# A diffusion transformer block with 32 experts on one core: an eighth ring area for the weight stream, and GpSimd's four DMAs on ScalarE's queue

## The chip, the core and the metric

The kernel runs on one core of one Trainium2 chip. A core has five engines with queues of their own: TensorE (PE in the profile; PEld is its weight loads), VectorE (DVE), ScalarE (ACT), GpSimd (POOL) and SyncE (SP), which here only issues DMAs. They work on the on-chip memory SBUF (128 partitions) and on the accumulators in PSUM; 16 DMA engines move data between SBUF and the memory outside. The metric is the device time of one execution in microseconds, lower is better.

## What is computed

One block on 256 tokens with 1024 features, in float32: modulation vectors from a condition, attention of two kinds over the tokens and 256 context tokens, and then a mixture of 32 experts. Cut to what matters here:

```python
sh1, sc1, g1, sh2, sc2, g2 = split(silu(c) @ w_mod + b_mod, 6)
h  = modulate(rms_norm(x, norm1_g), sh1, sc1)
p  = h @ w_in                              # q, k, v and gates; k and v of the context too
x  = x + g1 * merge_branches(global_attn(...), window_attn(...), gates, w_br_a, w_br_b, w_o)
h2 = modulate(rms_norm(x, norm2_g), sh2, sc2)
logits = h2 @ w_router + b_router          # top 4 of 32, softmax over the four: combine
for e in range(32):
    u = h2 @ w_e1[e] + b_e1[e]             # 1024 x 2048
    u_glu, u_lin = minimum(u[:, 0::2], 7), clip(u[:, 1::2], -7, 7)
    act = u_glu * sigmoid(1.702 * u_glu) * (u_lin + 1)
    out = out + combine[:, e:e+1] * (act @ w_e2[e] + b_e2[e])    # 1024 x 1024
return rms_norm(x + g2 * out, final_g)
```

The weights of the experts are 32 x 12 MB of float32, and each is read once.

## The kernel before, in words

Everything is one program in an order written out by hand. All large weights go through one **stream**: the list `pieces` names them in the order of their use, each piece a block of 128 partitions by 8 KB (1024 KB in all; half of that for `w_q`), an expert being eight pieces of `w1` and four of `w2`. `areas` holds `N_PAIR` SBUF tiles `ring0`, `ring1` and so on, of 16 KB per partition; each is two halves, and a half takes one piece. `pump` (L85 to L112) issues pieces on SyncE's queue as long as a half is in the list `spare`; `done` puts the half of a used piece back at the list's end and pumps again. So a piece's DMA waits, on SyncE, for the last reader of the piece whose half it takes, and SyncE works strictly in the order of the list. After attention two more tiles, `xx` and `ptt`, are free and join the areas (`grow`), four halves more.

The stages, with their use of the stream: the first modulation products and the q projection (`w_m0`, `w_q`), the other projections with the modulation sums on VectorE, GpSimd and ScalarE (`w_in`, `w_mod`; `mod_v`, `mod_p`, `mod_a`), attention head by head, the merge of the branches (`w_br`, `br_prod`), the output projection with the router's statistics (`w_o`, L692 to L723), the router (L732 to L793), and then the experts: `gather` picks the up to 64 tokens of an expert by a matmul, `gemm1` multiplies with `w1`, `act` computes the activation on VectorE and ScalarE in `tmp4`, `act_turn` transposes it, `gemm2` multiplies with `w2`, its result is scaled by `g2` (a row of 1024 numbers that stands in all partitions), and `scatter` adds it to the tokens. The matmuls of expert `e+1` start before those of `w2` of expert `e`. `settle` (L906) adds the experts' output biases `be2` once, during expert 5. The last two experts have an order of their own, in halves; among them stands a branch (`tc.If`, L1017) with a second path for experts that are chosen by more than 64 tokens. The final norm uses the row `fg`.

Small things have other queues. ScalarE's queue loads constants, x once more (L620), the router's weights and the biases `be1`. GpSimd's queue has four DMAs, for which its descriptors take a scratch in SBUF: `g2`, computed across partitions as `g2t` (8 x 128), is written to memory (L645) and read back as one row into all partitions (L726, into `r_kv`, 128 x 1024); `be2` (L729, into `mtx`, 128 x 512) and `fg` (L730, 128 x 1024) are loaded. In the queue of an engine a DMA stands among its computations, in program order.

DMAs of SyncE and ScalarE signal their end on eight semaphores, DMAHW0 to DMAHW7, given out in turn over both queues; a DMA waits until the one that had its semaphore before has landed, so at most eight are in flight. GpSimd's have others (DMASW).

Three small uses of a 2 KB buffer with the tag `msb` belong to the change: the products `bt` in `settle` and in the branch's path, and `g2x`, the two halves of `g2` put on top of each other for the last experts.

Of the kernel before, what the change touches and what calls it, by code (L numbers as in the profile page):

```python
# [7 lines left out]
F32 = mybir.dt.float32  # L8
# [13 lines left out]
LIMIT = 7.0  # L22
BIG = 1024.0
LOW = -3.0e38
N_PAIR = 7


C_ID, C_IOTA, C_SEL, C_BD2, C_COS, C_SIN, C_TRI, C_MK, C_END = 0, 128, 192, 194, 196, 452, 708, 836, 1092
# [6 lines left out]
def tile_dit_block(ctx: ExitStack, tc: tile.TileContext, xcT, consts, small, rows,  # L35
                   w_m0, w_q, w_mod, w_in, w_br, w_o, w_r, w1, b1, w2, b2, out):
    nc = tc.nc
    ctx.enter_context(tc.manual_schedule())
    per = ctx.enter_context(tc.tile_pool(name="per", bufs=1))
# [36 lines left out]

    areas = [per.tile([128, 4096], F32, name=f"ring{i}") for i in range(N_PAIR)]
    spare = [(i, h) for i in range(N_PAIR) for h in range(2)]
    n_next = [0]
    held, place = {}, {}  # L80

    def half(a):
        return areas[a[0]][:, 2048 * a[1]:2048 * a[1] + 2048]
# [482 lines left out]
    g2_dram = dram.tile([1, 1024], F32, name="g2_dram")  # L566
# [17 lines left out]
    for u in range(8):  # L584
        for qt in range(2):
# [9 lines left out]
            else:  # L595
                for m in (2 * qt, 2 * qt + 1):
                    tag, bufs = (("mm", 1), ("s", 2))[m % 2]
# [44 lines left out]
    nc.tensor.transpose(gp2[0:8, 0:128], modb[:, 24:32], ident)  # L642
    g2t = moe.tile([8, 128], F32, name="g2t", tag="SW", bufs=1)
    nc.vector.tensor_copy(g2t, gp2[0:8, 0:128])
    nc.gpsimd.dma_start(out=g2_dram.rearrange("o (b p) -> (o b) p", b=8), in_=g2t)  # L645
    g1h = moe.tile([128, 8], F32, name="g1h")
    nc.vector.tensor_scalar(out=g1h, in0=modb[:, 0:8], scalar1=0.5, scalar2=None, op0=ALU.mult)
    sh2 = modb[:, 8:16]
# [74 lines left out]
    stats(*pend)  # L723
    g2, fg = r_kv[:, 0:1024], r_kv[:, 1024:2048]
    tmp4 = r_q.rearrange("p (a c) -> p a c", a=4)
    nc.gpsimd.dma_start(out=g2, in_=g2_dram[0:1, :].to_broadcast([128, 1024]))  # L726

    be2 = mtx[:, 0:2, :].rearrange("p a b -> p (a b)")
    nc.gpsimd.dma_start(out=be2, in_=b2)  # L729
    nc.gpsimd.dma_start(out=fg, in_=rows[0:1, 1024:2048].to_broadcast([128, 1024]))  # L730

    nc.scalar.activation(out=junk, in_=eps, func=AF.Exp)  # L732
    u0 = bias1(0)
# [40 lines left out]
    x_t, y_t = t8[0].rearrange("p (a c) -> p a c", a=2), [t8[1].rearrange("p (a c) -> p a c", a=2)]  # L774
# [113 lines left out]
    def scatter(p, tbs=(0, 1)):  # L888
        t, y = TT[p], YY[p]
        for tb in tbs:  # L890
            for h in range(2):
                s = slice(512 * h, 512 * h + 512)
                sp = ps2.tile([128, 512], F32, name="sp", tag="sp", bufs=2)
                nc.tensor.matmul(sp, t[:, tb, :], y[:, s], start=True, stop=True)  # L894
                nc.vector.tensor_tensor(out=ACC[0][:, tb, s], in0=ACC[0][:, tb, s], in1=sp, op=ALU.add)  # L895
# [10 lines left out]
    def settle():  # L906

        ctp = ps2.tile([128, 512], F32, name="ctp", tag="tp")
        cw = mtx[:, 2, :].rearrange("p (a b) -> p a b", a=2)
        combT = mtx[:, 3, :]  # L910
        nc.gpsimd.memset(cw, 0.0)
        for h in range(2):
            nc.gpsimd.tensor_copy(cw[:, :, 64 * h:64 * h + 32], comb)
        for tb in range(2):
            nc.tensor.transpose(ctp[:, 128 * tb:128 * tb + 128], cw[:, tb, :], ident)
        nc.vector.tensor_copy(combT, ctp[:, 0:256])
        for tb in range(2):
            for h in range(2):
                s = slice(512 * h, 512 * h + 512)
                bp = ps2.tile([128, 512], F32, name="bp", tag="xg", bufs=2)  # L920
                nc.tensor.matmul(bp, combT[64 * h:64 * h + 64, 128 * tb:128 * tb + 128], be2[64 * h:64 * h + 64, :], start=True, stop=True)
                t = per.tile([128, 512], F32, name="bt", tag="msb")
                nc.vector.tensor_tensor(out=t, in0=bp, in1=g2[:, s], op=ALU.mult)
                nc.vector.tensor_tensor(out=ACC[0][:, tb, s], in0=ACC[0][:, tb, s], in1=t, op=ALU.add)

# [24 lines left out]
    for e in range(NE - 2):  # L950
        p, j = divmod(e, 2)
# [47 lines left out]
    aT = act_turn(e0)  # L999
    half1(0, 1, u)  # L1000
    scatter(NE // 2 - 2, (1,))
    g2x = per.tile([128, 512], F32, name="g2x", tag="msb")
    for h in range(2):
        nc.vector.tensor_copy(g2x[64 * h:64 * h + 64, :], g2[64 * h:64 * h + 64, 512 * h:512 * h + 512])
    gemm2(e0, aT)
# [11 lines left out]
    with tc.If(cnt > CAP):  # L1017
# [9 lines left out]
        slots = [half(s) for s in spare]  # L1027
# [10 lines left out]
        def body(e):  # L1038
# [11 lines left out]
            for tb in range(2):  # L1050
                aT = y_t[0][:, tb, :].rearrange("p (k s) -> p k s", k=8)
                for ch in range(4):
# [4 lines left out]
                    t = tmp4  # L1057
# [19 lines left out]
            for tb in range(2):  # L1077
                aT = y_t[0][:, tb, :].rearrange("p (k s) -> p k s", k=8)
                for h in range(2):
                    s = slice(512 * h, 512 * h + 512)  # L1080
                    y = ps2.tile([128, 512], F32, name="yd", tag="y")
                    for k in range(8):
                        nc.tensor.matmul(y, aT[:, k, :], vs[k // 2][:, k % 2, s], start=(k == 0), stop=(k == 7))
                    t = per.tile([128, 512], F32, name="bt", tag="msb")
                    nc.vector.tensor_tensor(out=t, in0=y, in1=g2[:, s], op=ALU.mult)
                    nc.vector.scalar_tensor_tensor(out=ACC[0][:, tb, s], in0=t, scalar=cv[:, tb:tb + 1],
                                                   in1=ACC[0][:, tb, s], op0=ALU.mult, op1=ALU.add)

        with tc.For_i(0, NE, 1) as e:
            body(e)  # L1090
# [144 lines left out]
```

## Time and profile before

| | us |
|---|---|
| median of 3 runs (lowest, highest) | 1224.25 (1223.93, 1226.63) |
| the profiled execution, its own time | 1224.82 |
| its span | 1223.0 |
| TensorE busy | 1159.1 (95%) |
| VectorE, ScalarE, GpSimd busy | 359.1, 138.8, 35.2 |
| moved by DMA | 458.36 MB, of it 454.06 MB on SyncE's queue |

The span is from the first to the last instruction of the profiled execution; 1.82 us of its time lie around it. A busy TensorE is not TensorE at its peak, since the ends of its matmuls are modelled. In the views below, L835 is line 835 of the kernel, `PE u L835` is the engine, the tile written and the line, an arrow points from what waited to what ended its wait, and a number in brackets behind an event is the idle time of its engine just before it. PEq, SPq and ACTq are the instruction queues of these engines, where DMA issues and branches appear.

### The profile page before, as it was taken

Reading aid. Unit: us, or ns where it says so; the run is one execution under the profiler, and the core shown is the slowest. Engines: PE = TensorE matmul, PEld = TensorE weight load, DVE = VectorE, ACT = ScalarE, POOL = GpSimd, SP = SyncE. Lnnn points to the kernel's source line nnn. Section 1 sums busy time; section 2 is a strip of 40 time slices with the busy share of each in tenths; the row PEclk is TensorE's granted clock in tenths of the full one; section 3 lists DMA queues with packets and bytes.
Section 4 is the critical chain, followed back from the end, with each engine's and each line's share of the span. In section 5 each row is a group of like instructions: output and inputs, shape, how many; then the busy total and the mean of one; then the engine's idle time right before and its main releaser. Section 6 shows DMA issues by size and latency. Waiting matters only on the chain. (4 is left out here: it accounts for less than half of the span.)

```text
span 1223.0 us, 13639 instructions
## 1 busy us (share of the span) xinstructions
PE 1159.1 (95%) x5624; PEld 529.7 (43%) x5624; DVE 359.1 (29%) x765; ACT 138.8 (11%) x304; POOL 35.2 (3%) x29
## 2 busy tenths in 40 slices
PE   7999999999999999999999999999999899999987
PEld 5888666883343334343434323232323232323222
DVE  3263665332222242322222222222222222222212
ACT  2122553030000000000000000000000000000002
POOL 0231100000000000000000000000000000000000
PEclk9999999999999999999999999999999999999997
DMA  9976655838999999999999999999999999999992
GB/s 379 377 296 212 235 206 201 342 134 361 422 421 421 421 420 421 421 421 421 421 421 422 421 421 421 421 421 421 421 421 421 420 421 421 421 421 421 414 391 75
DMA packets 70066, 458.36 MB, mean 375 GB/s; under 512 B 7848, under 2 KB 8240, under 8 KB 16752
## 3 DMA queue, kind: packets, MB, share of 16 engines
q1 hardware_dynamic: 68304, 454.06, 90.9%
q10 hardware_dynamic: 1296, 2.06, 0.5%
q0 software_dynamic: 400, 1.32, 0.3%
q8 instruction: 46, 0.75, 0.2%
q14 instruction: 20, 0.16, 0.0%
HBM read 456.36 MB, written 1.05 MB: 374 GB/s over the span
## 5 line engine op out<-in xcount | busy, mean ns | idle before, releaser
L835 PE MATMUL u<-ring,t 128*64 128x512 f32 x1488 | 346.0, 600 | 21.7 <-DMA ring<-w 21.7
L835 PEld LDWEIGHTS u<-ring,t 128*64 128x64 f32 x1488 | 99.5, 137 | 223.8 <-issue 162.9
L871 PE MATMUL y<-ring,r_q 128*64 128x512 f32 x832 | 184.2, 593 | 0.0
L884 DVE TENSOR_TENSOR t<-y,r_kv 64x512 f32<-64x512 f32 x60 | 41.3, 689 | 325.6 <-PE y L871 325.2
L871 PEld LDWEIGHTS y<-ring,r_q 128*64 128x64 f32 x832 | 59.3, 137 | 119.6 <-issue 115.8
L845 DVE TENSOR_SCALAR r_q<-u 128x512 f32<-128x512 f32 x31 | 21.4, 692 | 244.0 <-PE u L835 244.0
L835 PE MATMUL u<-ptt,t 128*64 128x512 f32 x320 | 75.6, 598 | 4.4 <-DMA ptt<-w 4.4
L847 ACT ACTIVATE r_q<-r_q 128x512 f32<-128x512 f32 x31 | 19.5, 630 | 505.8 <-DVE r_q L845 505.8
L688 PE MATMUL u<-mtx,keep 128*64 128x512 f32 x256 | 62.2, 604 | 3.0 <-DVE r_q L848 3.0
L805 PEld LDWEIGHTS xg<-mtx,r_y 128*128 128x128 f32 x512 | 58.4, 192 | 12.2 <-issue 12.2
L805 PE MATMUL xg<-mtx,r_y 128*128 128x128 f32 x512 | 61.3, 278 | 0.0
L368 PE MATMUL mm<-xx,ring 128*128 128x256 f32 x256 | 59.9, 385 | 0.0
L894 PE MATMUL sp<-t,mtx 128*128 128x512 f32 x120 | 59.7, 620 | 0.0
L368 PEld LDWEIGHTS mm<-xx,ring 128*128 128x128 f32 x256 | 47.3, 190 | 12.6 <-issue 5.0
L807 DVE TENSOR_TENSOR t<-xg,modb 128x512 f32<-128x512 f32 x32 | 22.1, 692 | 91.1 <-PE xg L805 91.1
L835 PE MATMUL u<-xx,t 128*64 128x512 f32 x176 | 40.4, 596 | 3.7 <-DMA xx<-w 3.7
L835 PEld LDWEIGHTS u<-ptt,t 128*64 128x64 f32 x320 | 21.6, 136 | 48.3 <-issue 34.4
L895 DVE TENSOR_TENSOR r_t<-r_t,sp 128x512 f32<-128x512 f32 x60 | 38.4, 681 | 5.1 <-PE sp L894 5.1
L894 PEld LDWEIGHTS sp<-t,mtx 128*128 128x128 f32 x120 | 20.5, 191 | 39.5 <-issue 39.5
L871 PE MATMUL y<-xx,r_q 128*64 128x512 f32 x160 | 36.3, 594 | 0.0
L688 PEld LDWEIGHTS u<-mtx,keep 128*64 128x64 f32 x256 | 16.3, 135 | 44.6 <-issue 22.6
L861 ACT COPY r_q<-ta 128x512 f32<-128x512 f32 x31 | 18.1, 585 | 145.5 <-PE ta L858 145.5
(245 smaller groups left out, 894.7 us busy)
## 6 DMA issues: line engine op xcount, KB each, us to landing
ring<-w SPq DMA_DIRECT2D x290, 1024.0 KB, 19.8
xx<-w SPq DMA_DIRECT2D x42, 1024.0 KB, 19.8
ptt<-w SPq DMA_DIRECT2D x40, 1024.0 KB, 19.8
ring<-w_mod SPq DMA_DIRECT2D x16, 1024.0 KB, 6.8
ring<-w_in SPq DMA_DIRECT2D x10, 1024.0 KB, 8.7
ring<-w SPq DMA_DIRECT2D x20, 512.0 KB, 11.8
ring<-w_m SPq DMA_DIRECT2D x8, 1024.0 KB, 12.5
ring<-w_q SPq DMA_DIRECT2D x8, 512.0 KB, 12.3
```

Of the source, the lines that this page charges most:

```text
L368: nc.tensor.matmul(gp[0][:, 0:256], w[:, k, :], x[:, k, :], start=(k == 0), stop=(k == 7))
L688: nc.tensor.matmul(u[c0:c0 + 64, ch % 2, :], ident[:, 4 * e + ch:4 * e + ch + 1].to_broadcast([128, 64]), be1, start=True, stop=False)
L805: nc.tensor.matmul(xp[:, b, :], z[:, tb, 128 * k:128 * k + 128], S[:, tb, :], start=(tb == 0), stop=(tb == 1))
L807: nc.vector.tensor_tensor(out=XT[p][:, 4 * h:4 * h + 4, :], in0=xp, in1=sh2[:, 4 * h:4 * h + 4].unsqueeze(2).to_broadcast([128, 4, 128]), ...
L835: nc.tensor.matmul(u[c0:c0 + 64, ch % 2, :], XT[p][:, k, 64 * j:64 * j + 64], w[:, 512 * ch:512 * ch + 512], start=False, stop=(k == 7))
L845: nc.vector.tensor_scalar(out=glu.rearrange("p (b f) -> p b f", b=2), in0=v[:, :, 0, :], scalar1=LIMIT, scalar2=None, op0=ALU.min)
L847: nc.scalar.activation(out=sg, in_=glu, func=AF.Sigmoid, scale=ALPHA)
L861: nc.scalar.copy(out=aT, in_=tp)
L871: nc.tensor.matmul(y[64 * h:64 * h + 64, :], l, w[:, 512 * h:512 * h + 512], start=(k == 0), stop=(k == 7))
L884: nc.vector.tensor_tensor(out=YY[p][64 * j:64 * j + 64, 512 * h:512 * h + 512], in0=y[64 * h:64 * h + 64, :], in1=g2[64 * h:64 * h + 64, 5 ...
L894: nc.tensor.matmul(sp, t[:, tb, :], y[:, s], start=True, stop=True)
L895: nc.vector.tensor_tensor(out=ACC[0][:, tb, s], in0=ACC[0][:, tb, s], in1=sp, op=ALU.add)
```

## The change

`N_PAIR` goes from 7 to 8, which gives the stream an eighth area of 16 KB per partition, so 16 halves in place of 14, and 20 in place of 18 with `xx` and `ptt`. The room comes from the scratch for GpSimd's descriptors, which the builder is told to make 1024 bytes, and from the `msb` buffer: `bt` in `settle` uses a quarter of `tmp4`, `g2x` half a row of `y_t`, and `bt` in the branch's path a free slot of the ring. GpSimd's four DMAs are issued on ScalarE's queue at the same places of the program.

```diff
--- before.py
+++ after.py
@@ -22,7 +22,7 @@
 LIMIT = 7.0
 BIG = 1024.0
 LOW = -3.0e38
-N_PAIR = 7
+N_PAIR = 8
 
 
 C_ID, C_IOTA, C_SEL, C_BD2, C_COS, C_SIN, C_TRI, C_MK, C_END = 0, 128, 192, 194, 196, 452, 708, 836, 1092
@@ -642,7 +642,7 @@
     nc.tensor.transpose(gp2[0:8, 0:128], modb[:, 24:32], ident)
     g2t = moe.tile([8, 128], F32, name="g2t", tag="SW", bufs=1)
     nc.vector.tensor_copy(g2t, gp2[0:8, 0:128])
-    nc.gpsimd.dma_start(out=g2_dram.rearrange("o (b p) -> (o b) p", b=8), in_=g2t)
+    nc.scalar.dma_start(out=g2_dram.rearrange("o (b p) -> (o b) p", b=8), in_=g2t)
     g1h = moe.tile([128, 8], F32, name="g1h")
     nc.vector.tensor_scalar(out=g1h, in0=modb[:, 0:8], scalar1=0.5, scalar2=None, op0=ALU.mult)
     sh2 = modb[:, 8:16]
@@ -723,11 +723,11 @@
     stats(*pend)
     g2, fg = r_kv[:, 0:1024], r_kv[:, 1024:2048]
     tmp4 = r_q.rearrange("p (a c) -> p a c", a=4)
-    nc.gpsimd.dma_start(out=g2, in_=g2_dram[0:1, :].to_broadcast([128, 1024]))
+    nc.scalar.dma_start(out=g2, in_=g2_dram[0:1, :].to_broadcast([128, 1024]))
 
     be2 = mtx[:, 0:2, :].rearrange("p a b -> p (a b)")
-    nc.gpsimd.dma_start(out=be2, in_=b2)
-    nc.gpsimd.dma_start(out=fg, in_=rows[0:1, 1024:2048].to_broadcast([128, 1024]))
+    nc.scalar.dma_start(out=be2, in_=b2)
+    nc.scalar.dma_start(out=fg, in_=rows[0:1, 1024:2048].to_broadcast([128, 1024]))
 
     nc.scalar.activation(out=junk, in_=eps, func=AF.Exp)
     u0 = bias1(0)
@@ -919,7 +919,7 @@
                 s = slice(512 * h, 512 * h + 512)
                 bp = ps2.tile([128, 512], F32, name="bp", tag="xg", bufs=2)
                 nc.tensor.matmul(bp, combT[64 * h:64 * h + 64, 128 * tb:128 * tb + 128], be2[64 * h:64 * h + 64, :], start=True, stop=True)
-                t = per.tile([128, 512], F32, name="bt", tag="msb")
+                t = tmp4[:, 0, :]
                 nc.vector.tensor_tensor(out=t, in0=bp, in1=g2[:, s], op=ALU.mult)
                 nc.vector.tensor_tensor(out=ACC[0][:, tb, s], in0=ACC[0][:, tb, s], in1=t, op=ALU.add)
 
@@ -999,7 +999,7 @@
     aT = act_turn(e0)
     half1(0, 1, u)
     scatter(NE // 2 - 2, (1,))
-    g2x = per.tile([128, 512], F32, name="g2x", tag="msb")
+    g2x = y_t[0][:, 1, 0:512]
     for h in range(2):
         nc.vector.tensor_copy(g2x[64 * h:64 * h + 64, :], g2[64 * h:64 * h + 64, 512 * h:512 * h + 512])
     gemm2(e0, aT)
@@ -1081,7 +1081,7 @@
                     y = ps2.tile([128, 512], F32, name="yd", tag="y")
                     for k in range(8):
                         nc.tensor.matmul(y, aT[:, k, :], vs[k // 2][:, k % 2, s], start=(k == 0), stop=(k == 7))
-                    t = per.tile([128, 512], F32, name="bt", tag="msb")
+                    t = slots[10][:, 0:512]
                     nc.vector.tensor_tensor(out=t, in0=y, in1=g2[:, s], op=ALU.mult)
                     nc.vector.scalar_tensor_tensor(out=ACC[0][:, tb, s], in0=t, scalar=cv[:, tb:tb + 1],
                                                    in1=ACC[0][:, tb, s], op0=ALU.mult, op1=ALU.add)
@@ -1225,7 +1225,7 @@
     from concourse.bass_utils import run_bass_kernel_spmd
 
     arrays = _pack(inputs)
-    nc = bacc.Bacc("TRN2", target_bir_lowering=False, num_devices=1)
+    nc = bacc.Bacc("TRN2", target_bir_lowering=False, num_devices=1, dynamic_dma_scratch_size=1024)
     args = [nc.dram_tensor(n, arrays[n].shape, F32, kind="ExternalInput").ap() for n in _ORDER]
     args.append(nc.dram_tensor("out", (256, 1024), F32, kind="ExternalOutput").ap())
     with tile.TileContext(nc) as tc:
```

What this does to the queues shows at two places. The first is SyncE's queue where the stream passes from the projections to the experts. A row is a DMA's target and source with its waits, `ring2_64` being area 2; `w1` and `w2` are expert pieces. Before, the four pieces that take the places of `w_o`, and then the first that take a place back from expert 0:

```order
L111 DMA ring1_63<-w1 128x2048 [waits DMAHW4_49,PE_49]
L111 DMA ring2_64<-w1 128x2048 [waits DMAHW5_49,PE_49]
L111 DMA ring4_66<-w1 128x2048 [waits DMAHW6_49,PE_49]
L111 DMA ring5_67<-w1 128x2048 [waits DMAHW7_49,PE_49]
L111 DMA ring2_64<-w1 128x2048 [waits DMAHW0_49,PE_49]
L111 DMA ring3_65<-w1 128x2048 [waits DMAHW1_49,PE_49]
L111 DMA ring6_68<-w1 128x2048 [waits DMAHW2_49,PE_49]
```

With the change, from the same release on:

```order
L111 DMA ring6_68<-w1 128x2048 [waits DMAHW7_49,PE_49]
L111 DMA ring0_62<-w1 128x2048 [waits DMAHW0_49,PE_49]
L111 DMA ring7_69<-w1 128x2048 [waits DMAHW1_49,PE_49]
L111 DMA ring0_62<-w1 128x2048 [waits DMAHW2_49,PE_49]
L111 DMA ring1_63<-w1 128x2048 [waits DMAHW6_49,PE_49]
L111 DMA ring3_65<-w1 128x2048 [waits DMAHW7_49,PE_49]
L111 DMA ring2_64<-w2 128x2048 [waits DMAHW0_49,PE_49]
L111 DMA ring1_63<-w2 128x2048 [waits DMAHW1_49,PE_49]
L111 DMA ring4_66<-w2 128x2048 [waits DMAHW2_49,PE_49]
L111 DMA ring2_64<-w2 128x2048 [waits DMAHW3_49,PE_49]
L111 DMA ring5_67<-w1 128x2048 [waits DMAHW4_49,PE_49]
L111 DMA ring4_66<-w1 128x2048 [waits DMAHW5_49,PE_49]
```

Each of the two begins with a piece that waits for the same matmuls of `w_o`. Before, the fifth row (`ring2_64` with DMAHW0) is the first to take a place from expert 0, the 19th expert piece of the queue; now it is also the fifth (`ring1_63` with DMAHW6), and it is the 21st. In its last three rows the semaphores DMAHW3, 4 and 5 were last given to three DMAs of ScalarE.

The second place is the end of the router's statistics (L679, L682), where the three loads stood on GpSimd's queue and now stand on ScalarE's. Before, on GpSimd:

```order
L645 DMA g2_dram_717<-g2t_1396 8x128 [waits DVE_49]
L726 DMA r_kv_72<-g2_dram_717 128x1024 [waits DMASW0_49,PE_49]
L729 DMA mtx_1349<-b2 128x512 [waits PE_49,Activation_49,Pool_49]
L730 DMA r_kv_72<-rows 128x1024
L755 TENSOR_SCALAR nm_1633<-top8_1632 128x2 [waits DVE_49]
```

and on ScalarE, with nothing between the last copy of `z` and the table load:

```order
L679 ACTIVATE rt_1448<-rl_1347,eps_110 128x2 [waits PE_49]
L682 COPY r_y_73<-tz_1613 128x2x128 [waits PE_49]
L732 ACT_TABLE_LOAD
L732 ACTIVATE junk_115<-eps_110 128x1
L745 COPY r_t_74<-tx_1650 128x512 [waits PE_49]
```

With the change, on ScalarE:

```order
L679 ACTIVATE rt_1451<-rl_1350,eps_113 128x2 [waits PE_49]
L682 COPY r_y_74<-tz_1616 128x2x128 [waits PE_49]
L726 DMA r_kv_73<-g2_dram_720 128x1024
L729 DMA mtx_1352<-b2 128x512 [waits DMAHW4_49,Activation_49]
L730 DMA r_kv_73<-rows 128x1024 [waits DMAHW5_49]
L732 ACT_TABLE_LOAD
L732 ACTIVATE junk_118<-eps_113 128x1
L745 COPY r_t_75<-tx_1653 128x512 [waits PE_49]
```

The three loads came between the copy at L682 and the table load at L732, ahead of the copies at L745; `be2` and `fg` wait for the earlier DMAs with semaphores DMAHW4 and DMAHW5. The write of `g2t` (L645) moves in the same way to ScalarE, between the load of `be1` (L629) and the first square (L706), where it waits for DMAHW3 and for VectorE.

## Rows read from the trace of the kernel before

**Rows 1.** The page's 40 slices of the span: bytes moved, GB/s

```profile
GB/s 379 377 296 212 235 206 201 342 134 361 422 421 421 421 420 421 421 421 421 421 421 422 421 421 421 421 421 421 421 421 421 420 421 421 421 421 421 414 391 75
```

**Rows 2.** Stretches: us, busy per engine, TensorE's granted clock, DMA share, GB/s

```profile
240.00:268.00 28.00, 27.99 (x160) 25.04 (x160) 9.73 (x26) 5.26 (x16) 0.00 (x0) 1.00 0.36 128
268.00:272.00 4.00, 3.66 (x31) 2.39 (x28) 3.08 (x19) 2.87 (x6) 1.30 (x3) 1.00 0.92 357
272.00:277.00 5.00, 5.00 (x41) 4.01 (x41) 2.01 (x9) 2.69 (x6) 0.00 (x0) 1.00 0.02 6
277.00:280.00 3.00, 3.00 (x18) 1.01 (x14) 1.93 (x10) 0.00 (x0) 0.00 (x0) 1.00 0.44 117
280.00:690.00 410.00, 405.34 (x1902) 151.02 (x1898) 103.70 (x193) 21.20 (x38) 0.72 (x3) 1.00 1.01 421
690.00:1158.00 468.00, 438.19 (x2020) 154.89 (x2016) 105.24 (x198) 21.20 (x38) 0.00 (x0) 1.00 1.01 421
```

**Rows 3.** Waits of PE, 276 to 690 us: total, times, longest us

```profile
PE u L688 <- DVE r_q L848: 3.0, 2, 1.5
PE bp L921 <- DVE bt L923: 1.2, 2, 0.8
```

**Rows 4.** Waits of PE, 690 to 1160 us

```profile
PE u L835 <- DMA ring<-w: 21.7, 41, 1.8
PE u L835 <- DMA ptt<-w: 4.4, 8, 0.6
PE u L835 <- DMA xx<-w: 3.7, 6, 0.9
```

**Rows 5.** The tail: events of PE in time [idle before], then two stretches

```profile
1156.33 1.94 PE L835 MATMUL u<-xx,t 128*64 128x512 f32 x8 [0.57 <-DMA xx<-w]
...
1191.20 3.68 PE L970 MATMUL u<-ring,t 128*64 128x512 f32 x8 [4.71 <-PEq L1017]
...
1190.00:1203.00 13.00, 11.80 (x24) 3.42 (x26) 0.75 (x2) 0.29 (x1) 0.00 (x0) 0.50 0.44 164
1203.00:1206.00 3.00, 2.54 (x14) 0.76 (x12) 0.85 (x3) 1.98 (x4) 0.00 (x0) 0.99 0.00 0
```

**Rows 6.** Events in time around 277 us: ScalarE, its queue, SyncE's queue

```profile
213.27 0.48 ACTq L624 DMA_DIRECT2D mtx<-w_r  x1
...
237.90 0.42 ACT L706 ACTIVATE sqs<-r_q 128x256 f32<-128x256 f32 x1 [23.15 <-DVE r_q L701]
...
267.74 0.37 ACT L682 COPY r_y<-tz 128x256 f32<-128x256 f32 x1
268.13 1.28 ACT L732 ACT_TABLE_LOAD   x1
...
270.73 2.05 ACT L745 COPY r_t<-tx 128x512 f32<-128x512 f32 x4 [1.10 <-PE tx L744]
...
277.48 0.33 SPq L111 DMA_DIRECT2D ring<-w  x1
...
286.59 0.33 SPq L111 DMA_DIRECT2D ring<-w  x1
```

**Rows 7.** DMA issues: count, KB each, us from issue to landing

```profile
ring<-w SPq DMA_DIRECT2D x290, 1024.0 KB, 19.8
...
mtx<-b ACTq DMA_DIRECT2D x1, 256.0 KB, 13.5
...
g_dram<-g2t POOLq DMA_DIRECT2D x1, 4.0 KB, 5.7
```

**Rows 8.** Events of GpSimd's queue, 205 to 272 us

```profile
224.79 0.73 POOL L645 DMA_DIRECT2D g_dram<-g2t  x1 [90.82 <-DVE a L650]
231.04 0.57 POOL L726 DMA_DIRECT2D r_kv<-g_dram  x1 [5.52 <-DMA g_dram<-g2t]
```

**Rows 9.** Waits of PE, 80 to 280 us

```profile
PE y L542 <- DVE r_y L552: 4.7, 6, 1.7
```

**Rows 10.** Waits of SyncE's queue, 20 to 140 us

```profile
SPq L111 <- DMA t<-consts: 14.0, 1, 14.0
```

## Prediction

> **What bounds the kernel now.** I read the page's slices first, then busy time by stretches, then who waits for whom, and last the order of events around one moment, 277 us, and in the tail. The slices [rows 1] show a transfer rate that moves between 134 and 379 GB/s in the first nine slices, some 275 us, and after one of 361 stands at 420 to 422 GB/s until the last three. The stretches [rows 2] say what that means. From 240 to 268 us the 16 DMA engines are 36% busy and from 272 to 277 us they are 2% busy, while TensorE is busy all the time: every place of the ring holds a weight piece that has not been used yet, so the stream stands still. From 280 us on the DMA share is 1.01 with 421 GB/s, in the first part (280 to 690 us) as in the second (690 to 1158 us).
>
> In the first of these two parts TensorE is the later one: it is busy 405.34 of 410 us, and no DMA is among the three things that it waited for there; the longest is 3.0 us for VectorE [rows 3]. In the second part it is busy only 438.19 of 468 us, and the gap of 29.8 us is what it waited for weight pieces: 21.7 + 4.4 + 3.7 us [rows 4]. So the stream is never idle after 280 us, TensorE catches up with it by about 690 us, and from there to about 1157 us the stream alone sets the pace. The last wait for a piece of an ordinary expert is at 1156.33 us [rows 5]; behind it comes a tail in TensorE's own order.
>
> The reader should take from this that time is lost to the stream only before 277 us, and that what counts is **how many pieces have been loaded when it starts again for good**.
>
> **The change, part by part.**
>
> *One more area.* The stream has 14 half areas of its own, and four more once `xx` and `ptt` join: 18 pieces of 1024 KB. With eight areas it has 20. In the order of SyncE's queue the first piece that needs a place given back by expert 0 is the 19th expert piece before, and the 21st now; both wait for the same matmuls. In the trace this piece is issued at 277.48 us [rows 6]. From there on the queue gets its releases at the same times as before, as long as TensorE runs as before, but each release issues a piece that stands two further on in the stream. The DMA engines are full from 280 us to the end, so the end of the stream moves by the time of two pieces. A piece is 1024 KB [rows 7], 1.0486 MB, and at 421 GB/s [rows 2] takes 2.49 us; eight of them in flight land 19.8 us after their issue [rows 7], 2.48 us each, which is the same number. Two pieces: **4.98 us**. The room to load them is there: two pieces cost 5 of the 28 us from 240 us on, in which the engines are 36% busy, and TensorE is not touched by it.
>
> TensorE must be able to use the lead. It needs longer to catch up, since two more pieces lie ready at 277 us; afterwards it still has 29.8 - 5.0 = 24.8 us of waits left. The lead is therefore kept to 1157 us, which becomes about 1152 us, and the tail follows with the same distances.
>
> Here the Trainium skill has another price: "DMA: Bandwidth & Descriptors", section "Where 436 GB/s comes from", says that for loads from HBM a limit of about 358 GB/s per core binds; by it two pieces would be 5.86 us and the result some 0.9 us lower. The trace disagrees with it for this core, 421 GB/s over 878 us, so the row's price is used.
>
> *Four loads and stores from GpSimd's queue to ScalarE's.* The write of `g2t` was issued at 224.79 us [rows 8], and is waited for by the first square on ScalarE at 237.90 us [rows 6] (the same buffer). The trace has 5.7 us for its landing, and 13.5 us for the slowest load of ScalarE's own queue [rows 7]. It has 13.1 us: cost nothing, by the worse row 0.4 us, and that square is added only a matmul group later. ScalarE has nothing else to do behind its wait in this time: it idles 23.15 us before that square [rows 6].
>
> The three loads (512, 256 and 512 KB) now stand on ScalarE between the last copy of `z` (267.74 us) and the table load (268.13 us) [rows 6]. The nearest price of an issue there is 0.48 us [rows 6], three make 1.4 us. Below them wait the table load, then four copies at 270.73 us, before which ScalarE idles 1.10 us for TensorE [rows 6]; the copies free the PSUM that expert 0's gather needs. So 1.4 - 1.1 = 0.3 us at most can reach the gather, and since the first of the three can be issued while the copy runs I take 0.1 us. This delay would move the start at 277.48 us, so it counts in full. A gain is possible too (GpSimd's next operation no longer stands behind two issues), but that operation came on time: zero. Their 1.25 MB take 3.0 us at 421 GB/s, and must fit into the 10 us from 267 to 277 us, of which the 5 us from 272 us were empty [rows 2]; the load of `g2`, moved from 231.04 us [rows 8] into this place, is the only addition and takes 1.2 us. Nothing.
>
> *The three buffers of 2 KB.* Bias products of `settle` go through `tmp4`, which VectorE writes next for the activation; it does both itself in the same order as before. `g2x` takes half of a `y_t` row whose last reader is two experts back. The overflow branch isn't taken in the profiled run: TensorE stands only 4.71 us at it [rows 5]. Nothing for each; if `tmp4` were still read, `settle` would wait up to the 1.2 us that VectorE's products there already cost TensorE [rows 3], in the stretch where TensorE, not the stream, is late but has 25 us in hand.
>
> *Scratch.* No software DMA is left that would use it. Nothing.
>
> *The front.* From 80 to 280 us no wait of TensorE is for a piece; the longest in sum is 4.7 us for VectorE [rows 9]. So earlier pieces shift nothing there. GpSimd gets its `w_mod` pieces earlier, which bounds a gain of under 1 us that I don't count.
>
> **Sum.** 1223.0 - 4.98 + 0.1 = 1218.1 us of span; with the 1.82 us around it that is 1219.9 us against the profiled execution's own 1224.82. That execution stands 0.57 us above the median of 1224.25, and from the median the sum is 1219.4. I forecast **1219.5 us**; its own range is 1217.0 to 1221.5, the scatter of the runs before (2.7 us from lowest to highest) around it.
>
> **The rivals.**
>
> *The tail's clock.* From 1190 to 1203 us TensorE is granted 0.50 of full speed (1.2 of 2.4 GHz), after it stood 4.71 us at the branch [rows 5]; it is busy 11.80 us there. The lead moves this place by 5 us. If the clock stayed full, half of the 11.80 us would come back: 1213.6 us. If it stayed low for the next 3 us as well, the 2.54 us busy there [rows 5] would double: 1222.0 us. For either: what follows is close to the kernel's end, where nothing hides it. Against: the idle time in front of it doesn't change. 5% and 7%.
>
> *No gain.* The pieces could be hidden anyway, if TensorE rather than the stream set the end: 1224.3 us. The 29.8 us of waits after 690 us [rows 4] speak against it; for it, that only a trace in which TensorE waits less would show what else is close behind. 6%.
>
> *Slower: the eight semaphores.* SyncE's and ScalarE's DMAs share eight completion semaphores in turn, and the three loads take three of them, just ahead of the new pieces: the sixth, seventh and eighth piece after the start wait until `g2`, `be2` and `fg` have landed, and the whole stream stands behind them. Such a hold is in the trace: SyncE stood 14.0 us for a load of constants that ScalarE had issued late [rows 10]. The sixth piece's turn is the release at 286.59 us [rows 6]. Five pieces in flight since 277.48 us carry the engines to about 292 us, so it decides from a landing after 288 us or so; a hold as long as the 14.0 us would leave the engines dry for some 9.6 us: 1219.5 + 9.6 = 1229.1 us. Against it: the loads are issued by about 269 us, and even 13.5 us [rows 7] bring the last to 282.6 us. 5%. The Trainium skill ("DMA: Bandwidth & Descriptors", "Anatomy of one DMA") says that a semaphore wait of a DMA happens on the issuing sequencer before dispatch; the 14.0 us agree, and by this rule a late load would hold everything behind it on SyncE, as priced here.
>
> **How the numbers follow.** The forecast has 77%, the rivals 5, 7, 6 and 5%. The range runs from 1217.0 to 1223.0: nearly all of the forecast and most of the low clock that lasts longer; no gain, the full clock and the hold stay outside. About 0.2%, 2.4 us, can be told from no change here, so faster is below 1221.8 and slower above 1226.7. Faster: 77 + 5 + 2 (the better part of the longer low clock) = 84%. Same: 5 + 6 = 11%. Slower: 5%.
>
> **What the new profile would show.** Right: the DMA engines at 421 GB/s from 280 us to an end about 5 us earlier, a piece issued by SyncE at 277.5 us as before, TensorE full until about 735 us in place of 690 (an estimate: from 277 to 690 us it used 18 + 413/2.49 = 184 pieces, 2.245 us each, so with 20 in front of it it meets the stream after 20/(1/2.245 - 1/2.49) = 456 us), its waits for pieces smaller by about 5 us, GpSimd's software queue gone. Wrong: the first issue after 277.48 us moved by more than 0.5 us, a second empty stretch of the DMA engines around 288 to 300 us with SyncE waiting for `r_kv` or `mtx`, or new waits of TensorE between 280 and 690 us. A span shortened by much more or less than 5 us with all this in place would have its cause in the tail, between 1152 us and the end.

## The result, and the profile after

The changed kernel took 1215.62 us (median of 5 runs, 1214.78 to 1217.09) against 1223.93 us (5 runs, 1221.46 to 1226.63) for the kernel before on the same chip: a ratio of 0.9934, interval 0.9916 to 0.9953. That is faster, as forecast, but by 8.3 us instead of 4.7; the time lies 1.4 us below the forecast's range. In a later lot with more runs (below) the same two kernels stood at 0.9962 (0.9946 to 0.9978), 1216.03 against 1221.18 us.

The profiled execution took 1215.62 us, its span is 1213.8 us, 9.2 less than before. First its stretches (columns as in [rows 2]):

```profile
272.00:277.00 5.00, 5.00 (x36) 3.16 (x36) 3.19 (x15) 1.62 (x3) 0.00 (x0) 1.00 0.07 25
277.00:280.00 3.00, 3.00 (x18) 1.00 (x16) 0.75 (x4) 0.00 (x0) 0.00 (x0) 1.00 0.82 295
280.00:690.00 410.00, 404.99 (x1908) 151.39 (x1906) 103.65 (x193) 21.20 (x38) 0.72 (x3) 1.00 1.01 420
...
690.00:720.00 30.00, 30.00 (x152) 12.28 (x148) 6.62 (x10) 1.22 (x2) 0.00 (x0) 1.00 1.01 421
...
690.00:1150.00 460.00, 433.61 (x2002) 154.05 (x1996) 105.18 (x198) 21.20 (x38) 0.00 (x0) 1.00 1.01 421
...
720.00:740.00 20.00, 18.94 (x84) 6.16 (x82) 7.12 (x16) 1.59 (x3) 0.00 (x0) 1.00 1.01 421
...
1184.00:1204.00 20.00, 16.89 (x58) 5.00 (x58) 4.38 (x10) 3.72 (x8) 1.87 (x2) 0.91 0.29 108
```

The picture of [rows 2] is still there: an empty place at 272 to 277 us, then full DMA engines at 420 to 421 GB/s to the end. From 690 to 720 us TensorE is busy throughout (30.00 of 30 us), and its first wait for a piece comes at 730.94 us: it meets the stream there, close to the forecast's 735 us. The forecast's 690 us for the kernel before was a bound of the stretches chosen, not an event: its first such wait comes at 696.24 us, the next at 726.06, and in three other executions with 14 halves the first comes at 724 to 725 us, in the three others with 16 at 748. So the distance of 45 us isn't confirmed. TensorE's waits from 690 to 1160 us, which answer to [rows 4], are still all for the stream:

```profile
PE u L835 <- DMA ring<-w: 22.0, 41, 1.7
PE u L835 <- DMA ptt<-w: 3.9, 7, 0.6
PE u L835 <- DMA xx<-w: 0.7, 2, 0.5
```

They sum to 26.6 us, 3.2 less than before, where 5 were forecast. The profiled execution of before has a stretch at a lower clock that this one hasn't:

```profile
420.00:440.00 20.00, 18.30 (x68) 5.86 (x67) 10.52 (x16) 0.63 (x1) 0.00 (x0) 0.91 1.01 421
```

A mean of 0.91 over 20 us is 3.6 us at 1.2 of 2.4 GHz, which cost TensorE half of that, 1.8 us, and 29.8 + 1.8 - 5.0 would be 26.6 us. But a second execution of the changed kernel (below) has the same stretch, 0.91, and its waits sum to 25.9 us, not to 24.8; and without the second path, where both kernels have it, they fall from 29.6 to 26.0 us. So with the clock alike the waits fall by 3.6 to 3.9 us, and the forecast's 5 was too much. The events that answer to [rows 5] and [rows 6], TensorE's, SyncE's and ScalarE's:

```profile
266.93 0.37 ACT L682 COPY r_y<-tz 128x256 f32<-128x256 f32 x1
266.93 0.35 ACTq L726 DMA_DIRECT2D r_kv<-g_dram  x1
267.38 0.38 ACTq L729 DMA_DIRECT2D mtx<-b  x1
267.80 0.44 ACTq L730 DMA_DIRECT2D r_kv<-rows  x1
268.28 1.28 ACT L732 ACT_TABLE_LOAD   x1 [0.98 <-ACT r_y L682]
269.68 2.03 ACT L745 COPY r_t<-tx 128x512 f32<-128x512 f32 x4
...
274.33 1.08 PE L835 MATMUL u<-ring,t 128*64 128x512 f32 x4
276.31 0.33 SPq L111 DMA_DIRECT2D ring<-w  x1
...
285.41 0.33 SPq L111 DMA_DIRECT2D ring<-w  x1
...
1150.44 1.94 PE L835 MATMUL u<-ring,t 128*64 128x512 f32 x8 [0.58 <-DMA ring<-w]
...
1185.29 3.55 PE L970 MATMUL u<-ring,t 128*64 128x512 f32 x8 [4.69 <-PEq L1017]
```

Between these events the 9.2 us divide into three:

| stretch of the profiled executions | before | after | difference |
|---|---|---|---|
| start to the first expert product (L835) | 275.51 | 274.33 | -1.18 |
| from there to the last wait for an ordinary piece | 880.82 | 876.11 | -4.71 |
| from there to the end | 66.67 | 63.36 | -3.31 |

The middle line is the lead, 4.71 us against a forecast of 4.98. The other two were forecast as zero (+0.1).

### The profile page after: what moved, and what is told of

Same layout as the page of the kernel before. It is cut to its first block, busy times and chain, and to the rows that moved or that the text cites. A ratio compares the mean times of both kernels' runs of the same rounds, so it can differ in the third digit from the quotient of the medians.

```text
span 1213.8 us, 13637 instructions
## 1 busy us (share of the span) xinstructions
PE 1152.5 (95%) x5624; PEld 528.7 (44%) x5624; DVE 360.9 (30%) x765; ACT 138.7 (11%) x304; POOL 32.7 (3%) x25
## 5 line engine op out<-in xcount | busy, mean ns | idle before, releaser
L835 PE MATMUL u<-ring,t 128*64 128x512 f32 x1600 | 369.9, 598 | 22.2 <-DMA ring<-w 22.0
L835 PEld LDWEIGHTS u<-ring,t 128*64 128x64 f32 x1600 | 107.5, 137 | 241.5 <-issue 179.5
L871 PE MATMUL y<-ring,r_q 128*64 128x512 f32 x784 | 174.0, 593 | 0.0
L871 PEld LDWEIGHTS y<-ring,r_q 128*64 128x64 f32 x784 | 55.9, 137 | 112.9 <-issue 107.1
L835 PE MATMUL u<-ptt,t 128*64 128x512 f32 x192 | 44.3, 596 | 3.9 <-DMA ptt<-w 3.9
L835 PE MATMUL u<-xx,t 128*64 128x512 f32 x192 | 45.2, 599 | 0.7 <-DMA xx<-w 0.7
L269 PE MATMUL qa<-xx,ring 128*128 128x256 f32 x128 | 30.7, 388 | 0.0
L698 PE MATMUL o<-r_t,ring 128*128 128x256 f32 x128 | 28.9, 380 | 0.0
```

The costliest lines, as they stand in the source:

```text
L269: nc.tensor.matmul(qa[c // 4][:, c % 4, :], w[:, 128 * c:128 * c + 128], x[:, j, :], start=(j == 0 and c % 2 == 0), stop=(j == 7), skip_gr ...
L698: nc.tensor.matmul(ps[:, 0:256], w[:, k, :], M[:, k, :], start=(k == 0), stop=(k == 7))
L835: nc.tensor.matmul(u[c0:c0 + 64, ch % 2, :], XT[p][:, k, 64 * j:64 * j + 64], w[:, 512 * ch:512 * ch + 512], start=False, stop=(k == 7))
L871: nc.tensor.matmul(y[64 * h:64 * h + 64, :], l, w[:, 512 * h:512 * h + 512], start=(k == 0), stop=(k == 7))
```

## The experiments

Theory A: the areas give the lead and a little in the front, and the rest is where TensorE's low clock fell in the few runs compared. Its rivals: the queue move gives the rest (B), or the whole 8 to 9 us belongs to the change and would be there again (C; in a later form T).

**The queue move alone.** `N_PAIR` back to 7, the rest as changed; only `bt` in the second path, which isn't taken, is back in its own buffer.

```diff
-N_PAIR = 8
+N_PAIR = 7
...
-                    t = slots[10][:, 0:512]
+                    t = per.tile([128, 512], F32, name="bt", tag="msb")
```

> Seven areas as before, but the four DMAs on ScalarE's queue, the small scratch and the reused 2 KB buffers as in the change. Theory A (the time went in three places: two pieces of lead 4.7 us, an earlier start of the stream 1.2 us of which 0.4 us from taking the loads off GpSimd, and 2 to 3 us from a shorter stretch of low clock in the tail, which differs from run to run whatever the kernel): 0.4 to 0.8 us below before, 1223.1 to 1223.5, with a first piece after the standstill issued between 276.6 and 277.1 us and the last wait for an ordinary piece at about 1155.5 us. Theory B (the move of the queue gives what was not forecast, 3.5 us): about 1220.5 us.

Measured: 1222.78 us (12 runs, 1219.89 to 1226.44), ratio 1.0002 (0.9984 to 1.0019); the kernel before had 1221.65 us here (23 runs, 1219.66 to 1228.55). No gain shows. B's 3.5 us are excluded, so B falls; A's 0.4 to 0.8 us are too small to be told from nothing here. The scatter is the second finding: 9 us, where the forecast went by 2.7.

**Half the areas added.**

```diff
-    spare = [(i, h) for i in range(N_PAIR) for h in range(2)]
+    spare = [(i, h) for i in range(N_PAIR) for h in range(2)][:15]
```

> The change with one of the sixteen halves withheld, so 19 places for expert pieces. Theory A: half of the lead is gone, the last wait for an ordinary piece 2.4 to 2.5 us later than the change has it, at 1152.9 us, and the time 1218.0 us within the tail's scatter of 1.5 us. Theory C (the tail got shorter because of the lead itself, so a piece less costs part of the tail too): about 1219.8 us, half of the way back to before.

Measured: 1222.93 us (12 runs, 1219.40 to 1224.40), ratio 1.0001 (0.9987 to 1.0015): no gain, which no theory expected. In the profiled execution the last ordinary wait came at 1155.31 us, but the lead is there: 878.30 us from the first expert product. It was lost earlier, in attention, where one stretch of this execution shows TensorE at a lower clock, as neither before nor after has it at this place:

```profile
140.00:160.00 20.00, 17.94 (x108) 11.57 (x106) 11.97 (x24) 10.98 (x28) 0.00 (x0) 0.91 0.51 171
```

That bears on the profiled execution; the median of twelve it doesn't explain. So the tail had to be taken out.

**Both kernels without the second path.** The same lines are taken out of each.

```diff
-    cnt = nc.values_load(cint[0:1, 0:1], min_val=0, max_val=256)
-    with tc.If(cnt > CAP):
...
```

> The kernel before without the branch at L1017 and the second path behind it (experts chosen by more than 64 tokens are left out), so TensorE does not stand 4.7 us in the tail. Theory A: the clock does not fall in the tail, all runs within 1 us of each other, the tail behind the last wait for an ordinary piece 56 us in place of 66.7, about 1214 us. Theory C makes no other forecast here; what counts is the difference to the next kernel.

> The change without the branch and the second path. Theory A: the tail as long as in the kernel before without the branch, to 0.3 us; the difference of the two is the lead and the earlier start alone, 5.9 us (5.5 to 6.3), so about 1208 us. Theory C (the lead shortens the tail): a difference of 8.3 to 9.2 us as with the branch.

Measured: 1213.63 us (6 runs, 1212.59 to 1214.05), ratio 0.9927 (0.9904 to 0.9950), and 1208.07 us (6 runs, 1207.65 to 1208.56), ratio 0.9882 (0.9859 to 0.9905). The difference is 5.56 us, as A has it; C's 8 to 9 us fall. Without the branch both tails take 56.1 us, and the runs lie within 1.5 us of each other. So the branch costs the kernel before 8.0 us (1221.65 to 1213.63), and most of the scatter of these runs goes with it. It isn't the only source: the kernel with 12 halves below scatters over 7.9 us, without a standstill at the branch.

**The changed kernel again**, with no edit, beside the kernel before, in more runs.

> The changed kernel again, beside the kernel before on one chip, since the runs of the kernel before lay 9 us apart. Theory A (the change itself is worth the lead and the earlier start, 5.6 to 6 us, as the two kernels without the second path differ by 5.56 us; the rest of the 8.3 us was where the low clock fell in the few runs compared): ratio 0.9950 to 0.9957, runs scattered over more than 2 us, and a low-clock stretch behind the branch that is as long in some runs of this kernel as in runs of the one before. Theory T (the change also shortens the low-clock stretch behind the branch, every time): ratio 0.9930 to 0.9940, runs within 2.5 us of each other, and again no more than 3.5 us at low clock between the branch and the last products.

Measured: 1216.03 us (12 runs, 1214.14 to 1222.13) against 1221.18 us (17 runs, 1219.64 to 1224.82), ratio 0.9962 (0.9946 to 0.9978). T falls: neither its ratio nor its narrow scatter came. A's range of the ratio is missed too, but lies inside the interval. The runs fall into groups, six at 1214.1 to 1215.0 us, three at 1217.0 to 1217.3, three at 1220.0 to 1222.1; the mean granted clock of the first is 0.994 to 0.995, of the last 0.990 to 0.992. The profiled one, of the first group, has the same short low-clock stretch as the first profile:

```profile
1184.00:1204.00 20.00, 17.59 (x60) 5.49 (x61) 4.49 (x10) 3.72 (x8) 2.54 (x2) 0.92 0.25 92
```

The queue move alone, above, has the long one of the kernel before [rows 5], with 14 halves and a time between:

```profile
1184.00:1204.00 20.00, 14.85 (x36) 3.98 (x32) 1.60 (x4) 2.12 (x4) 0.00 (x0) 0.66 0.54 198
```

A mean of 0.66 over 20 us is 13.6 us at 1.2 of 2.4 GHz, one of 0.91 or 0.92 some 3.4 us; the profiled execution with 15 halves has 0.83 there, 6.8 us. No trace shows one kernel with both lengths: in the five traces the stretch is the shorter the more halves there are. That it changes from run to run is inferred from the times and mean clocks: the kernel before, whose profiled execution took 1224.82 us, also has runs down to 1219.64 us in this lot, 5.2 us less, and the tail with the long stretch is 3.3 us longer than with the short one (66.67 and 63.36 us).

**15 halves and the queue move, both without the second path**: the dose without the tail. The edits are those of the first two experiments, made in the changed kernel without these lines.

> The changed kernel with 15 of the 16 half areas and without the second path (experts with more than 64 tokens, which these inputs don't have, are left out). Theory A (2.1 us a half): 1210.2 us (1209.9 to 1210.7), 878.2 us from the first expert product to the last wait on an ordinary piece. Rival (an odd number of halves loses its gain, by the order of the areas or by what the shared semaphores hold): 1212.5 to 1213.6 us, 880 us.

> The queue move alone (14 halves, smaller scratch) without the second path (experts with more than 64 tokens, which these inputs don't have, are left out). Against 1213.63 us for the kernel before without that path: theory A (the move gives the 0.37 us of VectorE's delay in the router and no more) 1213.2 us (1212.8 to 1213.6), first piece after the standstill at 276.7 to 276.9 us. Rival (the move gives the whole earlier start of 1.2 us): 1212.4 us (1212.0 to 1212.7). Rival (nothing): 1213.6 us.

Measured: 1213.26 us (4 runs, 1212.56 to 1214.03), ratio 0.9929 (0.9908 to 0.9949), and 1214.02 us (4 runs, 1212.81 to 1214.69), ratio 0.9935 (0.9914 to 0.9955). The second shows no gain from the queue move either. The first misses A's 1210.2 us: of the 5.95 us between 14 and 16 halves (the kernel with 16 ran on another chip) the 15th brought 0.8. Its stretch from the first expert product is 878.89 us, between 880.14 (14 halves) and 876.15 (16), so the 15th half brought 1.25 us of the lead and the 16th 2.74. Its first expert product came at 275.54 us, 1.3 us later than with 14. Of that, 0.96 us lie before the first modulation products, a time that differs between two executions of one kernel too (12.32 and 11.83 us); 0.31 us are a longer wait of TensorE at L542, here with 14, 15 and 16 halves:

```profile
145.24 0.66 PE L542 MATMUL y<-keep,st 128*64 128x128 f32 x8 [1.56 <-DVE r_y L552]
...
146.50 0.66 PE L542 MATMUL y<-keep,st 128*64 128x128 f32 x8 [1.87 <-DVE r_y L552]
...
145.69 0.66 PE L542 MATMUL y<-keep,st 128*64 128x128 f32 x8 [1.25 <-DVE r_y L552]
```

So the lead comes with each half, though not in equal parts, and the odd half costs 0.3 us in the front of this execution. Why it waits longer there, and whether the late start belongs to it, is open.

The queue move also showed me an error of reading. In the first profile VectorE's L751 came without the idle of 0.47 us that it has before, and GpSimd had issued its loads just then, so I held these for the cause. With the loads on ScalarE and 14 halves the idle is still there:

```profile
266.49 0.17 DVE L747 RECIPROCAL rt<-rt 128x2 f32<-128x2 f32 x1 [1.44 <-ACT rt L679]
267.13 0.41 DVE L751 SCALAR_TENSOR_TENSOR lg<-rl,rt,mtx 128x32 f32<-128x32 f32 x2 [0.47 <-DVE rt L747]
```

**A short second path.** The path is kept, but its body is a loop over quarters of an expert, so that fewer of TensorE's products and transposes stand in the program: counted in the code, 44 instead of 128. The expectation below has 60 and 137, which the code doesn't give.

```diff
-        def body(e):
+        def body(e, ch, cv):
...
-                for ch in range(4):
...
         with tc.For_i(0, NE, 1) as e:
-            body(e)
...
+            with tc.For_i(0, 4, 1) as ch:
+                body(e, ch, cv)
```

> The changed kernel with the second path kept, but its body written as a loop over quarters of an expert, so that TensorE's part of it has 60 products and transposes in the program instead of 137. Theory F (TensorE stands still at the branch because the instructions behind a long body have to be fetched, 6.2 us of the trace, while the other engines branch in under 0.1 us): the branch costs TensorE under 1 us, no long low-clock stretch follows, 1208.5 us (1207.8 to 1210). Rival G (the wait is the test itself, whatever the body): idle of 4.7 us at the branch as before, 1215 to 1217 us. In between, if half the body halves the fetch: idle of 2 to 3 us, 1211 to 1213 us.

Measured: 1208.74 us (5 runs, 1207.76 to 1208.91), ratio 0.9888 (0.9871 to 0.9906): theory F, and a version that beats both kernels by 7 and 12 us. The branch on the queues of VectorE and TensorE, duration in ns, first of the changed kernel:

```profile
L1017 DVEq COMPARE_BRANCH  x1: 72/72/72, 1174.8 to 1174.8; - x1
L1017 PEldq COMPARE_BRANCH  x1: 6189/6189/6189, 1178.9 to 1178.9; - x1
```

and with the short path, with TensorE's first products behind it and the stretch of the tail:

```profile
L1017 DVEq COMPARE_BRANCH  x1: 72/72/72, 1174.1 to 1174.1; - x1
L1017 PEldq COMPARE_BRANCH  x1: 223/223/223, 1178.2 to 1178.2; - x1
...
1180.06 1.94 PE L970 MATMUL u<-ring,t 128*64 128x512 f32 x8 [0.16 <-PEq L1017]
...
1176.00:1184.00 8.00, 7.32 (x28) 2.29 (x28) 0.00 (x0) 0.74 (x2) 0.00 (x0) 1.00 1.05 384
```

The test itself is cheap on every engine; on TensorE alone the branch took 6.19 us, where the jump went over its long body. In each of the five profiled executions with this standstill one packet of a DMA queue that the profile calls instruction, q8, falls into it; in the three with the short path q8 moved none during the branch. First the changed kernel, 1182.5 to 1183 us (packets, MB, share of the 16 engines), then all that the instruction queues moved with the short path from 1176 to 1190 us:

```profile
q8 instruction: 1, 0.02, 14.4%
...
q14 instruction: 3, 0.02, 0.5%
```

The Trainium skill has such a wait in "Runtime: NRT & Kernel Launch", section "Instruction fetch mechanics": a taken branch whose target isn't among the instructions already fetched waits until they are. The trace agrees; the page gives no price, the row does.

**The same short path in the kernel before**, and, in the changed one, 12 halves:

```diff
-N_PAIR = 8
+N_PAIR = 6
```

> The kernel before with the short second path of the changed kernel's faster version, and nothing else: 14 half areas, four loads on GpSimd's queue. It asks what the change is worth where TensorE neither stands still at the branch nor runs slowly behind it. Against 1208.74 us for the changed kernel with the short path: theory A (the areas give 4.4 us behind the start of the stream and 0.7 us ahead of it, the rest is scatter) 1213.9 us (1213.4 to 1214.5). Theory T (part of the 8.3 us first found came from a shorter low-clock stretch and would be gone here, but the lead is smaller than thought): under 1212.5 us. If the full 8.3 us were the areas': 1217.0 us.

> The changed kernel with the short second path and 12 half areas instead of 16. Theory A (2.2 us a half from the first expert product to the last wait on an ordinary piece, 876 us with 16 halves and 880.3 with 14): 884.6 us for that stretch, and 1218.0 us in all (1217.0 to 1219.5). Rival (the two areas last added gain more than those before, since the first pieces then wait for the front anyway): 882 us or less, under 1216 us. Rival (fewer areas delay the front too, by more than 1 us): first expert product later than 275.5 us, over 1219.5 us.

Measured: 1215.28 us (6 runs, 1213.85 to 1215.93), ratio 0.9942 (0.9923 to 0.9960): 6.5 us above the changed kernel with that path (on another chip). It misses A's range by 0.8 us at the upper end and lies between A's 1213.9 and the 1217.0 of the third forecast; T's is farther off. And 1222.73 us (10 runs, 1219.80 to 1227.72), ratio 1.0006 (0.9990 to 1.0022): the stretch from the first expert product is 885.29 us (expected 884.6), but that product came only at 277.88 us, so the rival that fewer areas delay the front holds too (its 1219.5 us are exceeded as well). The two profiled executions have a low-clock stretch in the front, the kernel before from 20 to 40 us and the one with 12 halves from 140 to 160 us, which makes the front of these two executions some 1.7 us longer (half of the low-clock time):

```profile
20.00:40.00 20.00, 20.00 (x136) 14.89 (x129) 4.62 (x17) 1.49 (x4) 0.00 (x0) 0.94 0.88 350
...
1184.00:1204.00 20.00, 18.43 (x72) 5.62 (x70) 3.73 (x8) 4.26 (x9) 1.26 (x1) 1.00 0.66 246
```

```profile
140.00:160.00 20.00, 16.78 (x100) 11.03 (x98) 11.92 (x22) 10.53 (x26) 2.35 (x1) 0.91 0.47 162
```

**What the second path costs when it is taken.**

```diff
-CAP = 64
+CAP = 40
...
+    c[:, C_IOTA + 40:C_IOTA + 64] = 1000.0
```

> The changed kernel with the short second path, where an expert's first path holds 40 tokens instead of 64, so that the tokens above it take the second path: what that path costs when it is taken. Its loop has 128 turns with 3 MB of weights each; by the 421 GB/s of the stream alone that is 0.96 ms, and a turn also waits for its loads and products one after the other: 2500 us in all by an estimate of 10 us a turn, 2000 to 5000 us.

Measured: 7267 us in one run, far above the estimate: some 47 us for each of the 128 turns. TensorE alone is busy for 31 us of a turn (at a granted clock of 0.70 to 0.82 in two stretches of 100 us) and waits for 7 us for the turn's loads and 9 us for VectorE and ScalarE; the estimate had no room for its products. The long body wasn't run in this way, so whether the short one costs more there is open.

All profiled executions side by side, by events of the trace (us; * has a low-clock stretch in the front):

| kernel | halves | first modulation products (L228) | from there to the first expert product | from there to the last ordinary wait |
|---|---|---|---|---|
| 12, short path | 12 | 12.22 | 265.66* | 885.29 |
| before | 14 | 12.76 | 262.75 | 880.82 |
| before, no second path | 14 | 12.61 | 262.62 | 880.31 |
| before, short path | 14 | 12.97 | 264.28* | 880.26 |
| queue move | 14 | 12.17 | 262.75 | 880.15 |
| queue move, no second path | 14 | 11.56 | 262.69 | 880.14 |
| 15 | 15 | 12.05 | 264.96* | 878.30 |
| 15, no second path | 15 | 12.52 | 263.02 | 878.89 |
| after | 16 | 12.32 | 262.01 | 876.11 |
| after, again | 16 | 11.83 | 262.03 | 875.66 |
| after, no second path | 16 | 11.89 | 261.99 | 876.15 |
| after, short path | 16 | 11.90 | 262.06 | 875.78 |

## Why the prediction was right in its core and wrong in its number

- **The lead: right, and somewhat smaller.** The last column falls by 4.95 us from 12 halves to 14 (mean 880.34) and by 4.4 from 14 to 16 (mean 875.93); 4.98 was forecast for two. In the whole kernel 14 to 16 halves were worth 5.56 us where the branch doesn't disturb (both kernels without it, on one chip). The stream's rate after, 420 and 421 GB/s, is again above the 358 GB/s that the Trainium skill gives ("DMA: Bandwidth & Descriptors", "Where 436 GB/s comes from").
- **The front: sized wrong.** "So earlier pieces shift nothing there" fails by 0.7 us: all four executions with 16 halves need 262.0 to 262.1 us from the first modulation products to the first expert product, the four undisturbed ones with 14 need 262.6 to 262.8. About 0.3 us of it is a shorter wait of TensorE at L542 around 146 us (1.25 against 1.56 us, with the queue moved in both kernels), the rest the idle before VectorE's L751. The gain had been left out as "under 1 us that I don't count", with another cause (GpSimd's `w_mod`). Of the profiled pair's 1.18 us the other 0.44 lie before the first modulation products. Why more areas shorten the two waits isn't settled.
- **The queue move: right.** The forecast was 0.1 us, and neither pair of kernels shows a difference clear of its interval; by the table the time to the first expert product is 262.75 us with and without the move, and 262.69 against 262.62 without the second path. The three issues took 0.35, 0.38 and 0.44 us, and the first ran beside a copy; the 1.10 us that ScalarE had idled in front of L745 [rows 6] absorbed them, and the copies came without a wait at 269.68 us. `be2` and the 2 KB buffers didn't show. The first pieces after 276.31 us followed at their releases, the sixth at 285.41 us, so the hold by the eight semaphores did not occur.
- **The tail and the base: here the number failed.** The step that failed is "the tail follows with the same distances", which put the tail at nothing: in the profiled pair it got 3.31 us shorter, with some 3.4 us at 1.2 GHz behind the branch in place of 13.6. With it failed the base and the spread. The forecast took off its 4.9 us from 1224.25 us, the median of three runs, and took "the scatter of the runs before (2.7 us from lowest to highest)" for the spread. 57 later runs of the same kernel, on three chips, lie between 1218.81 and 1228.55 us, their medians in three lots at 1221.65, 1221.18 and 1220.91. The three runs stood 3 us above these. From 1221.2 us the same sum gives 1216.3; 1216.03 was measured. That this fits so well is in part luck: the lead came out 0.5 us smaller and the front 0.7 us shorter than forecast. Four comparisons give the change 5.15 us (the later lot), 5.56 (both without the second path), 5.95 (areas alone, without it) and 6.54 (both with the short one); the last two compare different chips. So of the 8.3 us some 5 to 6.5 are the change's. That the rest came with the sample is likely, not shown: on which chip the first lot ran isn't on record, so a difference of the chip isn't excluded.
- **The rival that was nearly right.** The low clock behind the branch was seen and priced (full clock 1213.6 us, 5%), but as an effect of the lead, and set aside with "the idle time in front of it doesn't change". That is true (4.71 and 4.69 us), and yet the stretch behind it was 13 us in one execution [rows 5] and 3.6 in the other. That it changes from run to run of one and the same kernel is what the three groups of the second lot and their mean clocks speak for; no trace shows it. The forecast should have taken this as the spread of the runs, on both sides of the comparison, and set its range's lower end by it: 3 us lower.
- **Smaller slips.** Five pieces issued "since 277.48 us" last to about 292 us; a hold until 286.59 + 14.0 = 300.6 us would by these numbers leave the engines dry for 8.6 us, not 9.6. The 1.25 MB of the three loads take 3.1 us at 421 GB/s, not 3.0. Neither changes the forecast.

## What to carry to other kernels

Where a stream that never rests sets the pace, more buffer is worth about the transfer time of what it holds, once, and it can be counted before it is built: two halves brought 4.4 to 5 us here, against 4.98 counted. A single one brought less than half of that. Where the profile shows a low clock of some ten us near the end, three runs are no base for a forecast: take the kernel's scatter from that stretch, and compare with it taken out. And look at a branch that is never taken by the length of what it jumps over, on each engine: here 84 fewer products and transposes in the program were worth 7.3 us in the changed kernel, more than the change itself.

## What the runs showed of the hardware

- A compare-and-branch took 45 to 72 ns on four engines and 6189 ns on TensorE, where it jumped over a body with 128 products and transposes; with 44 of them it took 223 ns, and 90 ns in the run that takes the short path, where TensorE doesn't jump. TensorE's idle time there fell from 4.69 to 0.16 us.
- All five profiled executions in which TensorE idled 4.7 to 4.9 us at the branch fell to 1.2 GHz behind it; of the seven in which it didn't, none did between this place and its last products. With the short path the time came down by 7.3 us in the changed kernel (1216.03 to 1208.74) and by 5.6 in the one before (1220.91 to 1215.28 on one chip), more than the idle itself.
- A stretch of some 3.4 us at 1.2 GHz also falls into other places: at 429 to 438 us in nine of the twelve executions, behind short idle times of TensorE (0.52, 0.78 and 0.40 us at L921), which the other three have as well without it; at 147 us in two, behind idle times of 2.06 and 2.88 us at L542; at about 740 us in three, and at 20 and 970 us in one each.
